# Memory key and value products, split by upper and lower 64 features onto two tiles of array rows

## The chip, the core and the metric

One core of a Trainium2 chip runs the whole program in one launch. The metric is the device time of that launch in microseconds (us). The kernel before takes 2544.36 us, the median of three runs (2544.34 to 2545.03).

## The reference, cut to what matters

The reference is a decoder trunk of four layers (256 positions, width 2048) that cycles through three attention mixers. Each layer also attends to a memory of 256 rows, whose keys and values come from one projection per layer. Only that projection is touched here:

```python
mem_n = _rmsnorm(mem, mem_norm)                       # (1, 256, 2048)
for i in range(DEPTH):                                # 4 layers
    ...
    mem_out = _memory_attention(mq, mem_n @ w_mem_kv[i])   # w_mem_kv[i]: (2048, 2048)
# first 1024 columns of the product: keys of 4 heads x 256; last 1024: values
```

## The kernel before

All numbers are 32-bit floats. Each operand of a large product is split into a high and a low part (`split`, L81: ScalarE makes the high part in the type `float32r`, VectorE subtracts it from the value for the low part), and a product is the sum of three: high by high, high by low, low by high. The contraction runs over 2048 features in 16 steps of 128, which are the 128 rows of TensorE's array.

`memory()` (L412 to L502) comes first and makes the keys and values of all four layers. For each layer and each half `p_` it makes one value product, then two key products:

- A value product (`rows_by`, L270) keeps memory features as the stationary operand and streams 512 columns of weights: six matmuls of 512 columns for each of 16 steps, into two PSUM banks (the tile `acc_mv`).
- A key product (`columns_by`, L294) keeps 128 weight columns as the stationary operand and streams the memory: for each step two matmuls of 512 columns (high weights by both parts of the memory, L310) and two of 256 (low weights by the high part, L314), into the two banks of `acc_mk`.

There are 8 value products and 16 key products. The first value product is special: it also prepares the memory's own parts while the first weights arrive.

Weights come by DMA in pieces of 512 KB (`stage`, L234, five buffers, issued on SP's queue). `parts_of` (L264) splits each piece of 128x512 into `wh` (ScalarE, L74) and `wl` (VectorE, L83), each with three buffers. TensorE reads them and so frees them. The kernel lays out eight PSUM banks: two pairs under the tag `acc` (one product fills a pair while the pair before is read out), and four single banks under the tag `mp` (`misc`, L57), which `memory()` uses only for `spread`.

When a key product ends, `keys` (L459) calls `total` (L341: ScalarE copies one half of each bank to `z`, VectorE adds the other), multiplies by a scale (L462), splits and sends the result to DRAM on GpSimd's queue. When a value product ends, `values` (L449) scales and splits it straight from PSUM. `spread` (L196) runs two small matmuls over all 128 rows: once for the memory's scales, and once, near the end of `memory()`, for the norm of layer 0.

Each engine works through its own queue in order. The framework's scheduler fixes that order when the program is built, by its own estimate of times, so that `wl` pieces for the next product stand between the steps that read out the last one.

Of the kernel before, what the change touches and what calls it, by code (L numbers as in the profile page):

```python
# [8 lines left out]
F32 = mybir.dt.float32  # L9
# [6 lines left out]
P = 128  # L16
S = 256
# [7 lines left out]
MEMW = 1024  # L25
ST = 2
N_TAB = 384
PQ, AUX, WR, PT, WARM = 5, 4, 5, 4, 11
# [17 lines left out]
def kernel(ctx: ExitStack, tc: tile.TileContext, a: dict, out: bass.AP,  # L46
                             kinds=(0, 1, 2, 0)):
    nc = tc.nc
# [3 lines left out]
    act = ctx.enter_context(tc.tile_pool(name="act", bufs=1))  # L52
    wk = ctx.enter_context(tc.tile_pool(name="wk", bufs=1))
    ps = ctx.enter_context(tc.tile_pool(name="ps", bufs=1, space=bass.MemoryType.PSUM))
    dr = ctx.enter_context(tc.tile_pool(name="dr", bufs=1, space=bass.MemoryType.DRAM))

    def misc(name, dt=F32):  # L57
        return ps.tile([P, 512], dt, name=name, tag="mp", bufs=4)
# [14 lines left out]
    def copy_act(o, i, scale=1.0):  # L73
        inst = nc.scalar.activation(o, i, AF.Copy, scale=scale)  # L74
        if pinned:
            tc.keep_in_program_order(inst)
# [182 lines left out]
    def other_work():  # L259
        for _ in range(2):  # L260
            if steps and next(steps[0], None) is None:
                steps.pop(0)

    def parts_of(wr, c0, n):  # L264
        wh = wp.tile([P, 512], F32R, name="wh", tag="wh", bufs=3)
        wl = wp.tile([P, 512], F32R, name="wl", tag="wl", bufs=3)
        split(wh[:, :n], wl[:, :n], wr[:, c0:c0 + n])
        return wh, wl

    def rows_by(xt, kts, w, k0, cols, name, prepare=None, each=None, exact_first=False):  # L270


        pair = ps.tile([P, 2, 512], F32, name=f"acc_{name}", tag="acc", bufs=2)
        acc = [pair[:, t, :] for t in range(2)]
        for s in range(0, kts, ST):
            m = min(ST, kts - s)
            wr, n = stage(w, k0 + s, m, cols, each)
            other_work()
            for k in range(m):
                if prepare is not None:  # L280
                    prepare(s + k)
                wh, wl = parts_of(wr, k * n, n)
                q = xt[(s + k) // 4]
                seq = [(t, v, w_) for t in range(2) for v, w_ in ((0, wh), (0, wl), (1, wh))]
                if exact_first:
                    seq.sort(key=lambda z: z[2] is wl)
                for n_, (t, v, w_) in enumerate(seq):
                    later = [z for z in seq[n_ + 1:] if z[0] == t]
                    nc.tensor.matmul(acc[t][:, :n], q[:, v, (s + k) % 4, t * P:(t + 1) * P], w_[:, :n],  # L289
                                     start=s + k == 0 and v == 0 and w_ is wh,  # L290
                                     stop=s + k == kts - 1 and not later)
        return pair

    def columns_by(xt, kts, w, k0, cols, name):  # L294

        pair = ps.tile([P, 2, 2, S], F32, name=f"acc_{name}", tag="acc", bufs=2)
        acc = [pair[:, j] for j in range(2)]
        for s in range(0, kts, 2 * ST):
            m = min(2 * ST, kts - s)
            wr, n = stage(w, k0 + s, m, cols)  # L300
            other_work()
            for k2 in range(0, m, 2):
                wh, wl = parts_of(wr, k2 * S, 2 * S)
                for k in range(2):
                    kt = s + k2 + k
                    q = xt[kt // 4]

                    for j in range(2):
                        o = k * S + j * P
                        nc.tensor.matmul(acc[j], wh[:, o:o + P], q[:, :, kt % 4, :],  # L310
                                         start=kt == 0, stop=False)
                    for j in range(2):
                        o = k * S + j * P
                        nc.tensor.matmul(acc[j][:, 0, :], wl[:, o:o + P], q[:, 0, kt % 4, :],  # L314
                                         start=False, stop=kt == kts - 1)
        return pair

    def columns_of(xt, kts, w, c0, tiles, name):
# [19 lines left out]
                                         q[:, 0, kt % 4, r0:], start=False, stop=kt == kts - 1)  # L338
        return pair, acc[2:]

    def total(pair, name="z"):  # L341
        z = tmp(name).rearrange("p (j c) -> p j c", j=2)
        copy_act(z, pair[:, :, 1, :])
        nc.vector.tensor_add(z, z, pair[:, :, 0, :])
        return z
# [66 lines left out]
    def memory():  # L412
        mrstd = cst.tile([P, 2], F32, name="mrstd")
        m16 = cst.tile([P, 2], F32, name="m16")
        mbc = act.tile([P, S], F32, name="mbc", tag="kr", bufs=1)
        mT = [act.tile([P, 2, 4, S], F32R, name="mT", tag=f"big{c}") for c in range(4)]
        mss = small("mss", 8, bufs=2)

        def each(k):

            if k == 1:
                mft[0].load(1)
            if k in (3, 7, 11):
                mft[k // 4 + 1].load(0, 4)
            if k == 15:
                tc.keep_in_program_order(nc.sync.dma_start(ident, a["c_ident"]))
                nc.vector.tensor_copy(identr, ident)

        def prepare(k):
            c = k // 4  # L430
            weighted_parts(mT[c], mft[c].q, k % 4, c * 4)

        def memory_rows(c):
            q = act.tile([P, 2, 512], F32, name="mrow", tag="pq", bufs=PQ)
            for t in range(2):
                tc.keep_in_program_order(
                    nc.sync.dma_start(q[:, t, :], min_[t][:, c * 512:(c + 1) * 512]))
            return q

        def row_scales(mrow):  # L440
            for c in range(4):
                for t in range(2):
                    square_sum(mss[:, t * 4 + c:t * 4 + c + 1], mrow[c][:, t, :])
            s2 = small("ms2", 2)
            nc.vector.tensor_reduce(s2, mss.rearrange("p (t c) -> p t c", t=2), AX.X, OP.add)
            rsqrt_mean(mrstd, s2, D)
            nc.vector.tensor_scalar(m16, mrstd, 0.0625, None, op0=OP.mult)

        def values(i, p_, acc):  # L449
            v = [act.tile([P, 2, 512], F32R, name="mv", tag="aux", bufs=AUX) for z in range(2)]  # L450
            for t in range(2):
                sc = mrstd[:, t:t + 1]
                copy_act(v[0][:, t, :], acc[:, t, :], scale=sc)
                nc.vector.scalar_tensor_tensor(v[1][:, t, :], acc[:, t, :], sc, f32(v[0])[:, t, :],
                                               op0=OP.mult, op1=OP.subtract)
            for z in range(2):
                nc.gpsimd.dma_start(mv[i][p_][:, z], v[z])

        def keys(i, h, acc):  # L459
            kT = act.tile([P, 2, 2, S], F32R, name="mkT", tag="pq", bufs=PQ)  # L460
            z = total(acc)
            nc.vector.tensor_mul(z, z, mbc[:, None, :].to_broadcast([P, 2, S]))  # L462
            split(kT[:, 0], kT[:, 1], z)
            nc.gpsimd.dma_start(mkT[i][h], kT)

        def first_keys(acc):
            yield True
            yield True
            spread(mbc, m16)
            keys(0, 0, acc)  # L470

        for i in range(depth):
            w = a["w_mem_kv"][i]
            for p_ in range(2):
                begins = i == p_ == 0
                if begins:

                    pinned.append(0)
                    acc = rows_by(mT, 16, w, 0, (MEMW, 512), "mv", prepare, each, True)
                    pinned.pop()  # L480
                    mrow = [memory_rows(c) for c in range(4)]
                    raw = act.tile([P, 2, 512], F32, name="raw", tag="aux", bufs=AUX)
                    for t in range(2):
                        copy_act(raw[:, t, :], acc[:, t, :])
                else:
                    values(i, p_, rows_by(mT, 16, w, 0, (MEMW + p_ * 512, 512), "mv"))
                for h in (2 * p_, 2 * p_ + 1):
                    acck = columns_by(mT, 16, w, 0, (h * 256, 256), "mk")
                    if begins and h == 0:
                        row_scales(mrow)  # L490
                        values(i, p_, raw)
                        steps.append(first_keys(acck))
                    else:
                        keys(i, h, acck)
                step = 2 * i + p_
                if begins:

                    not_before(f32(mT[3])[:, 0, 3, :1])
                    late_constants()
                    bias_tables()  # L500
                if 1 <= step < 5:
                    steps.append(nm.first_chunk(step - 1))  # L502
# [826 lines left out]
```

## Time and profile before

| | before |
|---|---|
| median of 3 runs | 2544.36 us |
| the profiled execution, whole | 2544.75 us |
| its span, first to last instruction | 2543.0 us |
| TensorE (PE) busy in the span | 2532.3 us, 100% |
| weight loads of the array (PEld) busy | 2184.4 us, 86% |
| VectorE (DVE) busy | 1889.3 us, 74% |
| ScalarE (ACT) busy | 1604.9 us, 63% |
| granted TensorE clock, mean | 0.999 |

PE is the matmul stream, PEld the loads of stationary operands, which the trace shows on a line of their own. Matmuls are pipelined: one lasts longer than the distance between two starts, so the cost of a matmul is read from starts, not from durations. An idle engine that nobody waits for costs nothing.

### The profile page before, as it was taken

The page shows a single profiled execution, that of the slowest core. Times are in us where ns is not written, and L with a number is a line of the kernel's source. Part 1 is how long each engine was busy: PE and PEld are TensorE (multiplying, and loading weights), DVE is VectorE, ACT ScalarE, POOL GpSimd, SP SyncE. Part 2 cuts the span into 40 slices and gives each one's busy share as a digit, 9 for nine tenths or more (in the row PEclk, how much of TensorE's full clock was granted, in tenths as well). Part 3 has the DMA queues.
Part 4 walks back from the last instruction along what each step waited for, and adds up shares of the span by engine and source line. Part 5 has one row for each costly group of instructions (what it writes and reads, how often), then busy time and mean ns, then how long its engine had stood idle before and what let it go on. Part 6 is the DMA issues. An engine that isn't in the chain of part 4 may idle for free.

```text
span 2543.0 us, 41598 instructions
## 1 busy us (share of the span) xinstructions
PE 2532.3 (100%) x14070; PEld 2184.4 (86%) x14070; DVE 1889.3 (74%) x3832; ACT 1604.9 (63%) x3291; POOL 95.9 (4%) x237
## 2 busy tenths in 40 slices
PE   9999999999999999999999999999999999999998
PEld 8888888888888889888888888888889888888887
DVE  6666666677777677988777777878868777777766
ACT  6556556556566556777666566667756666656655
POOL 1200000000000000000000000000000000000000
PEclk9999999999999999999999999999999999999999
DMA  9888777676677666766666565666656768666765
GB/s 306 258 265 259 248 213 236 174 190 179 184 191 208 198 194 192 216 188 176 191 186 186 170 219 176 178 179 176 197 157 176 227 185 221 191 193 188 220 172 185
DMA packets 478582, 511.67 MB, mean 201 GB/s; under 512 B 70656, under 2 KB 391040, under 8 KB 477728
## 3 DMA queue, kind: packets, MB, share of 16 engines
q1 hardware_dynamic: 461856, 451.82, 60.7%
q0 software_dynamic: 15792, 56.22, 7.0%
q8 instruction: 110, 1.80, 0.3%
q10 hardware_dynamic: 720, 0.98, 0.1%
q14 instruction: 104, 0.85, 0.1%
HBM read 483.67 MB, written 29.46 MB: 202 GB/s over the span
## 4 chain that ended last, share of the span: by engine, by line
PE 99%; DVE 0%; DMA 0%; ACT 0%; issue 0%; SPq 0%; DVEq 0%
PE acc_wo L289 20%; PE acc_g L310 14%; PE acc_g L314 7%; PE acc_mv L289 7%; PE acc_q L310 5%; PE acc_mq L310 5%; PE acc_mk L310 5%; PE acc_cq L310 4%; PE acc_qn L310 4%; PE acc_q L314 2%; PE acc_mq L314 2%; PE acc_mk L314 2%; PE acc_cq L314 2%; PE acc_qr L310 2%; PE acc_qn L314 2%; PE acc_va L289 2%
## 5 line engine op out<-in xcount | busy, mean ns | idle before, releaser
L74 ACT ACTIVATE wh<-wr 128x512 fp32r<-128x512 f32 (+1 forms) x1712 | 1064.9, 624 | 816.7 <-PE acc_g L310 143.3
L83 DVE TENSOR_TENSOR wl<-wr,wh 128x512 fp32r<-128x512 f32 (+1 forms) x1712 | 1155.0, 679 | 558.7 <-ACT wh L74 529.7
L310 PE MATMUL acc_g<-xT,wh 128*128 128x512 f32 x1536 | 483.8, 397 | 0.0
L289 PE MATMUL acc_wo<-wh,y 128*128 128x512 f32 x1504 | 473.1, 391 | 0.0
L314 PEld LDWEIGHTS acc_g<-xT,wl 128*128 128x128 f32 x1536 | 282.4, 188 | 62.7 <-DVE wl L83 0.9
L289 PEld LDWEIGHTS acc_wo<-wh,y 128*128 128x128 f32 x1504 | 282.4, 188 | 55.9
L314 PE MATMUL acc_g<-xT,wl 128*128 128x256 f32 x1536 | 304.8, 280 | 0.0
L289 PE MATMUL acc_wo<-wl,y 128*128 128x512 f32 x752 | 297.7, 396 | 0.0
L310 PEld LDWEIGHTS acc_g<-xT,wh 128*128 128x128 f32 x1536 | 235.4, 189 | 0.9
L289 PEld LDWEIGHTS acc_wo<-wl,y 128*128 128x128 f32 x752 | 141.3, 188 | 26.4
L310 PE MATMUL acc_q<-xT,wh 128*128 128x512 f32 x512 | 161.4, 396 | 0.0
L310 PE MATMUL acc_mq<-xT,wh 128*128 128x512 f32 x512 | 161.1, 396 | 0.0
L310 PE MATMUL acc_mk<-mT,wh 128*128 128x512 f32 x512 | 160.7, 395 | 0.0
L289 PE MATMUL acc_mv<-wh,mT 128*128 128x512 f32 x512 | 156.6, 390 | 1.7 <-ACT wh L74 1.7
L310 PE MATMUL acc_qn<-cT,wh 128*128 128x512 f32 x384 | 121.0, 396 | 0.0
L310 PE MATMUL acc_cq<-xT,wh 128*128 128x512 f32 x384 | 120.9, 396 | 0.0
L314 PEld LDWEIGHTS acc_mk<-mT,wl 128*128 128x128 f32 x512 | 95.8, 188 | 22.6 <-DVE wl L83 0.2
L289 PEld LDWEIGHTS acc_mv<-wh,mT 128*128 128x128 f32 x512 | 95.9, 188 | 22.2 <-ACT wh L74 2.7
L1248 DVE TENSOR_TENSOR xc<-xc,acc_wo 128x1024 f32<-128x1024 f32 x92 | 112.1, 1218 | 2.6 <-PE acc_wo L289 2.3
L314 PEld LDWEIGHTS acc_q<-xT,wl 128*128 128x128 f32 x512 | 94.7, 188 | 22.2 <-issue 0.7
L314 PEld LDWEIGHTS acc_mq<-xT,wl 128*128 128x128 f32 x512 | 94.8, 188 | 21.7 <-issue 0.2
L314 PE MATMUL acc_q<-xT,wl 128*128 128x256 f32 x512 | 102.2, 281 | 0.0
(332 smaller groups left out, 3833.2 us busy)
## 6 DMA issues: line engine op xcount, KB each, us to landing
wr<-in_w_out_dram SPq DMA_DIRECT2D x188, 512.0 KB, 3.8
wr<-in_w_in_a_dram SPq DMA_DIRECT2D x176, 512.0 KB, 4.3
wr<-in_w_mem_kv_dram SPq DMA_DIRECT2D x126, 512.0 KB, 4.7
wr<-in_w_in_b_dram SPq DMA_DIRECT2D x116, 512.0 KB, 3.6
wr<-in_w_in_c_dram SPq DMA_DIRECT2D x104, 512.0 KB, 3.5
wr<-in_w_uq_dram SPq DMA_DIRECT2D x288, 128.0 KB, 2.8
wr<-in_w_in_a_dram SPq DMA_DIRECT2D x32, 288.0 KB, 3.1
mv<-mv POOLq DMA_DIRECT2D x16, 512.0 KB, 6.6
```

What stands on the lines that cost most here:

```text
L74: inst = nc.scalar.activation(o, i, AF.Copy, scale=scale)
L83: nc.vector.tensor_sub(lo, src, f32(hi))
L289: nc.tensor.matmul(acc[t][:, :n], q[:, v, (s + k) % 4, t * P:(t + 1) * P], w_[:, :n], start=s + k == 0 and v == 0 and w_ is wh, stop=s + k ...
L310: nc.tensor.matmul(acc[j], wh[:, o:o + P], q[:, :, kt % 4, :], start=kt == 0, stop=False)
L314: nc.tensor.matmul(acc[j][:, 0, :], wl[:, o:o + P], q[:, 0, kt % 4, :], start=False, stop=kt == kts - 1)
L1248: nc.vector.tensor_add(xs, xs, acc)
```

## The change

Every value product but the first, and every key product, is cut in two over the contraction. Each matmul over 128 array rows becomes two matmuls over 64 rows: one at array rows 0 to 63, into the `acc` bank as before, and one at rows 64 to 127, into a bank of the tag `mp` (the tile `acb_...`). The same columns are streamed in both. At the end the two banks are added: for keys by four VectorE additions of 128x256 after `total`, for values by a ScalarE copy of both `acc` banks to a new tile `vr` and two VectorE additions of 128x512; `values` then reads `vr` instead of PSUM.

```diff
+    def row_halves(name, n):
+        pair = ps.tile([P, 2, 512], F32, name=f"acc_{name}", tag="acc", bufs=2)
+        banks = [pair[:, t, :] for t in range(2)], [misc(f"acb_{name}") for t in range(2)]
+
+        def product(t, l, r, start, stop):
+            width = r.shape[1] * (r.shape[2] if len(r.shape) == 3 else 1)
+            for z in range(2):
+                rows = slice(64 * z, 64 * z + 64)
+                nc.tensor.matmul(banks[z][t][:, :width], l[rows], r[rows], start=start, stop=stop,
+                                 tile_position=(64 * z, 0))
+        return pair, banks[1], product
+
+    def rows_in_halves(xt, kts, w, cols, name):
...
+                for t in range(2):
+                    for n_, (v, w_) in enumerate(((0, wh), (0, wl), (1, wh))):
+                        product(t, q[:, v, k % 4, t * P:(t + 1) * P], w_[:, :],
+                                k == n_ == 0, k == kts - 1 and n_ == 2)
+        return pair, more
+
+    def columns_in_halves(xt, kts, w, cols, name):
...
+                    for j in range(2):
+                        product(j, wh[:, k * S + j * P:k * S + j * P + P], q[:, :, kt % 4, :], kt == 0, False)
+                    for j in range(2):
+                        product(j, wl[:, k * S + j * P:k * S + j * P + P], q[:, 0, kt % 4, :],
+                                False, kt == kts - 1)
+        return pair, more
...
         def keys(i, h, acc):
-            z = total(acc)
+            z = total(acc[0].rearrange("p j (v c) -> p j v c", v=2))
+            for j in range(2):
+                for v in range(2):
+                    nc.vector.tensor_add(z[:, j, :], z[:, j, :], acc[1][j][:, v * S:(v + 1) * S])
...
-                    values(i, p_, rows_by(mT, 16, w, 0, (MEMW + p_ * 512, 512), "mv"))
+                    acc, more = rows_in_halves(mT, 16, w, (MEMW + p_ * 512, 512), "mv")
+                    vr = act.tile([P, 2, 512], F32, name="vr", tag="aux", bufs=AUX)
+                    copy_act(vr, acc)
+                    for t in range(2):
+                        nc.vector.tensor_add(vr[:, t, :], vr[:, t, :], more[t])
+                    values(i, p_, vr)
                 for h in (2 * p_, 2 * p_ + 1):
-                    acck = columns_by(mT, 16, w, 0, (h * 256, 256), "mk")
+                    acck = columns_in_halves(mT, 16, w, (h * 256, 256), "mk")
```

TensorE's queue at the start of the first key product, before: `acc_mk` is the pair of banks, `mT` the memory, `wh` and `wl` the parts of the weights, and the shape is that of the output.

```order
L310 MATMUL acc_mk_385<-mT_148,wh_388 128x512 x2
L314 MATMUL acc_mk_385<-mT_148,wl_389 128x256 x2
L310 MATMUL acc_mk_385<-mT_148,wh_388 128x512 x2
L314 MATMUL acc_mk_385<-mT_148,wl_389 128x256 x2
L310 MATMUL acc_mk_385<-mT_148,wh_400 128x512 x2
```

The same place after the change: `acb_mk` are the two further banks.

```order
L350 MATMUL acc_mk_385<-mT_148,wh_390 128x512
L350 MATMUL acb_mk_386<-mT_148,wh_390 128x512
L350 MATMUL acc_mk_385<-mT_148,wh_390 128x512
L350 MATMUL acb_mk_387<-mT_148,wh_390 128x512
L350 MATMUL acc_mk_385<-mT_148,wl_391 128x256
L350 MATMUL acb_mk_386<-mT_148,wl_391 128x256
L350 MATMUL acc_mk_385<-mT_148,wl_391 128x256
L350 MATMUL acb_mk_387<-mT_148,wl_391 128x256
```

Each matmul has become two that stand next to each other in the queue, one for each tile of rows; nothing else stands between them.

VectorE's queue where a key product ends and a value product begins (layer 0, last head), before: `z` is the tile that collects the keys, and the `wl` pieces are already those of the value product.

```order
L83 TENSOR_TENSOR wl_1194<-wr_1191,wh_1193 128x512
L344 TENSOR_TENSOR z_1156<-z_1156,acc_mk_1050 128x512
L462 TENSOR_TENSOR z_1156<-z_1156,mbc_147 128x512
L83 TENSOR_TENSOR wl_1204<-wr_1191,wh_1203 128x512
L83 TENSOR_TENSOR wl_1216<-wr_1213,wh_1215 128x512
```

The same place after the change.

```order
L83 TENSOR_TENSOR wl_1590<-wr_1587,wh_1589 128x512
L390 TENSOR_TENSOR z_1534<-z_1534,acc_mk_1362 128x512
L510 TENSOR_TENSOR z_1534<-z_1534,acb_mk_1363 128x256
L510 TENSOR_TENSOR z_1534<-z_1534,acb_mk_1364 128x256
L510 TENSOR_TENSOR z_1534<-z_1534,acb_mk_1363 128x256
L510 TENSOR_TENSOR z_1534<-z_1534,acb_mk_1364 128x256
L511 TENSOR_TENSOR z_1534<-z_1534,mbc_147 128x512
L83 TENSOR_TENSOR wl_1606<-wr_1587,wh_1605 128x512
```

The four additions have come between the third `wl` piece of the value product and the fourth. GpSimd's and SP's queues issue the same transfers; from layer 0's first product on, TensorE's queue is the same as before.

## Rows read from the trace of the kernel before

**Rows 1.** The page: busy time of the engines, and chain by engine.

```profile
PE 2532.3 (100%) x14070; PEld 2184.4 (86%) x14070; DVE 1889.3 (74%) x3832; ACT 1604.9 (63%) x3291; POOL 95.9 (4%) x237
...
PE 99%; DVE 0%; DMA 0%; ACT 0%; issue 0%; SPq 0%; DVEq 0%
```

**Rows 2.** Stretches: length, busy PE, PEld, DVE, ACT, POOL; clock, DMA share, GB/s.

```profile
52.36:74.14 21.78, 21.78 (x98) 18.02 (x97) 12.75 (x20) 11.14 (x18) 12.18 (x44) 1.00 0.83 259
74.14:96.43 22.29, 22.29 (x130) 19.45 (x128) 14.23 (x22) 12.36 (x21) 8.22 (x35) 1.00 0.87 266
...
140.48:361.01 220.53, 220.53 (x1125) 187.61 (x1123) 141.59 (x231) 125.61 (x216) 10.62 (x20) 1.00 0.79 248
361.01:2543.00 2181.99, 2174.08 (x12254) 1879.91 (x12252) 1656.43 (x3439) 1392.90 (x2917) 60.09 (x126) 1.00 0.66 191
```

**Rows 3.** Matmuls of both kinds of product by shape: count, busy us, mean ns.

```profile
L310 PE MATMUL acc_mk<-mT,wh 128*128 128x512 f32 x512 | 160.7, 395 | 0.0
L289 PE MATMUL acc_mv<-wh,mT 128*128 128x512 f32 x512 | 156.6, 390 | 1.7 <-ACT wh L74 1.7
L314 PE MATMUL acc_mk<-mT,wl 128*128 128x256 f32 x512 | 100.7, 278 | 0.0
L289 PE MATMUL acc_mv<-wl,mT 128*128 128x512 f32 x256 | 97.0, 389 | 0.0
```

**Rows 4.** Timeline of TensorE in a key product: start us, us, what.

```profile
130.03 0.63 PE L310 MATMUL acc_mk<-mT,wh 128*128 128x512 f32 x2
130.50 0.39 PE L314 MATMUL acc_mk<-mT,wl 128*128 128x256 f32 x2
130.73 0.63 PE L310 MATMUL acc_mk<-mT,wh 128*128 128x512 f32 x2
```

**Rows 5.** Timeline of the weight loads in the same stretch.

```profile
130.27 0.42 PEld L314 LDWEIGHTS acc_mk<-mT,wl 128*128 128x128 f32 x2
```

**Rows 6.** Matmuls on tiles of 64 array columns, layer 1's attention: mean ns.

```profile
L1081 PE MATMUL o<-pT,vs 128*64 128x384 f32 x64 | 13.2, 492 | 0.0
```

**Rows 7.** Timeline: two such matmuls, one on each tile.

```profile
1162.29 0.49 PE L1081 MATMUL o<-pT,vs 128*64 128x384 f32 x2
```

**Rows 8.** Timeline of TensorE into and out of these tiles.

```profile
1161.70 0.39 PE L314 MATMUL acc_q<-xT,wl 128*128 128x256 f32 x2
1162.02 0.44 PE L1081 MATMUL o<-pT,vh 128*64 128x128 f32 x4
1162.29 1.03 PE L1081 MATMUL o<-pT,vs 128*64 128x384 f32 x8
1163.15 0.61 PE L1081 MATMUL o<-pT,vh 128*64 128x128 f32 x8
1163.59 1.03 PE L1081 MATMUL o<-pT,vs 128*64 128x384 f32 x8
1164.45 0.39 PE L1081 MATMUL o<-pT,vh 128*64 128x128 f32 x4
1164.77 0.74 PE L310 MATMUL acc_q<-xT,wh 128*128 128x512 f32 x2
1165.35 0.40 PE L314 MATMUL acc_q<-xT,wl 128*128 128x256 f32 x2
```

**Rows 9.** Timeline of VectorE after a key product that ended at 140.48.

```profile
141.12 0.69 DVE L83 TENSOR_TENSOR wl<-wr,wh 128x512 fp32r<-128x512 f32 x1 [0.70 <-ACT wh L74]
141.73 0.68 DVE L344 TENSOR_TENSOR z<-z,acc_mk 128x512 f32<-128x512 f32 x1
142.44 0.69 DVE L462 TENSOR_TENSOR z<-z,mbc 128x512 f32<-128x512 f32 x1
143.05 0.69 DVE L83 TENSOR_TENSOR wl<-wr,wh 128x512 fp32r<-128x512 f32 x1
```

**Rows 10.** Timeline of TensorE: the matmul that first reads that last piece.

```profile
144.80 0.39 PE L289 MATMUL acc_mv<-wl,mT 128*128 128x512 f32 x1
```

**Rows 11.** An addition of 128x256 from PSUM elsewhere: count, busy us, mean ns.

```profile
L571 DVE TENSOR_TENSOR u<-sp,caus 128x256 f32<-128x256 f32 x32 | 13.4, 417 | 0.0
```

**Rows 12.** Timeline: two weight loads one after another, after the column tiles.

```profile
1164.77 0.30 PEld L310 LDWEIGHTS acc_q<-xT,wh 128*128 128x128 f32 x2 [0.17 <-issue]
```

More of the change, by code (lines that the diff above doesn't have):

```diff
@@ L339, in columns_of @@
         return pair, acc[2:]
+    def row_halves(name, n):
[9 more added lines that the diff above has]
+    def rows_in_halves(xt, kts, w, cols, name):
+        pair, more, product = row_halves(name, 512)
+        for s in range(0, kts, ST):
+            wr, n = stage(w, s, ST, cols)
+            other_work()
+            for k in range(s, s + ST):
+                wh, wl = parts_of(wr, (k - s) * n, n)
+                q = xt[k // 4]
+                for t in range(2):
[4 more added lines that the diff above has]
+    def columns_in_halves(xt, kts, w, cols, name):
+        pair, more, product = row_halves(name, 512)
+        for s in range(0, kts, 2 * ST):
+            wr, n = stage(w, s, 2 * ST, cols)
+            other_work()
+            for k2 in range(0, 2 * ST, 2):
+                wh, wl = parts_of(wr, k2 * S, 2 * S)
+                for k in range(2):
+                    kt = s + k2 + k
+                    q = xt[kt // 4]
+                    for j in range(2):
[4 more added lines that the diff above has]
+        return pair, more
     def total(pair, name="z"):
```

## The prediction, made before the changed kernel ran

> **What bounds the kernel now.** I read the page first. TensorE is busy for the whole span, and the chain that ended last lies on it for 99% [rows 1]. So time moves only where TensorE's own stream gets shorter, longer or is made to wait. Next comes the view by stretches. [...] VectorE has 12.8 to 14.2 us of work in such a stretch and ScalarE 11.1 to 12.4: both have room on the average. From layer 0's first product, at 361.01, nothing is changed on TensorE's queue, so the 2182 us after it stay [rows 2], and the question lies in the 309 us from the second value product on and in the first two key products.
>
> [...] The groups by shape give 768 matmuls for 8 value products, 96 each, and 1024 for 16 key products, 64 each [rows 3]. [...]
>
> [...] In the timeline of the loads, the first load for the low weights starts at 130.27, 0.01 us after the second of the matmuls that began at 130.03 (130.03 + 0.63 less one duration of 0.40, from the mean in [rows 3]), so it lies beside a whole matmul [rows 5]. [...]
>
> **The change, part by part.**
>
> *The products.* 7 x 96 + 16 x 64 = 1696 matmuls become 1696 pairs. No row shows tiles of array rows. The nearest rows are the tiles of array columns in layer 1's attention: one matmul of 384 columns lasts 492 ns [rows 6], and two of them, one on each tile, together 0.49 us from the first start to the last end [rows 7]: they run side by side. Eight matmuls (four of 384 columns, four of 128) lie between 1162.29 and 1163.15, and eight of 128 between 1163.15 and 1163.59 [rows 8]. That is 0.11 us per pair of 128 and (0.86 - 0.22) / 2 = 0.32 us per pair of 384. [...] One ns per pair is 1.7 us.
>
> *Changes between whole array and tiles.* Going in: from 1161.70 to 1162.29 there are two matmuls of 256 columns (0.23) and two pairs (0.22), yet 0.59 us pass: 0.14 is lost. Coming out: from 1164.45 to 1165.35, two pairs (0.22) and two matmuls of 512 (0.47) take 0.90: 0.21 is lost [rows 8]. The changed queue goes in after the first value product, out and in around the first `spread`, whose two matmuls stand together, out and in twice around the second, whose two stand apart, and out at layer 0: four times each way, 4 x 0.35 = 1.4 us. Bounds: 0 to 2.8, twice that.
>
> *Reading out a key product.* Here VectorE's room decides. Before, after a product that ended at 140.48, VectorE makes the third `wl` piece of the value product, adds, multiplies, and makes the fourth, ready at 143.05 + 0.69 = 143.74 [rows 9]; TensorE reads it at 144.80 [rows 10]. So 1.06 us are to spare. The change puts four additions of 128x256 in between. One takes 0.42 us [rows 11]. An instruction that does not read its predecessor's result starts 0.08 before its end (141.12 + 0.69 against 141.73), one that does 0.03 after it (141.73 + 0.68 against 142.44) [rows 9]. Three of the steps are of the first kind and the last, into the multiplication, is of the second: 3 x 0.34 + 0.45 = 1.47 us. That is 0.41 more than there is to spare, and TensorE, in order, stands still for it. There are seven such ends before a value product: 7 x 0.41 = 2.9 us. Bounds: 0.30 (all at 0.34) to 0.74 (all at 0.45) each, 2.1 to 5.2 us. Behind a key product followed by another key product, the order puts the multiplication after the fourth piece and the need comes later: nothing. Behind a value product the copy to `vr` and two additions of 0.68 (as L344 in [rows 9]) stand before the third `wl` piece. No row here gives the spare time; I bound it by 0 and the 0.74 of a key product's end, seven times 0 to 5.2 us, and take 0, as the copy falls while VectorE has nothing urgent. The banks themselves wait for nobody: the next product has the other pair and the other two of `mp`.
>
> *Sum.* Against the profiled execution, 2544.75 us (span 2543.0 and 1.75 around it; the median of the runs is 0.39 less): 2544.75 + 0 + 1.4 + 2.9 = 2549.05. I say **2549 us**, 0.2% over the median. About 0.2%, 5.1 us, is what a measurement of this kernel can tell from no change, so this stands near that edge.
>
> **Rivals.**
>
> [...]
> [...]
>
> *The two tiles' loads go one after another, or hold up both streams (slower).* A load occupies the array for 0.11 us: two in a row last 0.30, and one 0.19 (0.42 for two less the 0.23 between their starts) [rows 5, 12]. Two per pair are 0.22, less than a matmul of 512 columns, but 0.10 more than one of 256 (0.23 / 2 [rows 4]). It decides from the point where the two loads of a pair outlast its matmul: the 512 pairs of 256 columns, + 51 us, 2544.75 + 51 + 4.3 = 2600. [...] For it: twice as many loads in the same time. Against it: the column tiles also load twice per pair, within 0.11 us per pair of 128 [rows 8].
> [...]
>
> *The pairs do not run side by side at all* (the change does not do what it says): 7 x 21.78 + 8 x 22.29 = 331 us more, 2880. Against it speak the column tiles [rows 7].
>
> **How the numbers follow.** Pairs like single matmuls: 0.48, own range 2546 to 2554 (a ns per pair either way, the bounds of the stalls), about half of it within 0.2% of before and half above. Gap gone: 0.30, faster. Gap doubled: 0.10; loads in a row: 0.07; nothing side by side: 0.05; all slower. So faster 0.30, same 0.25, slower 0.45. The range leaves out the two dearest cases (0.12) and a part of the tails: 2526 to 2576.
>
> **What would show it.** [...] A load on one tile that starts only when the other's has ended shows the loads in a row. Idle time of TensorE before the fourth `wl` of each value product, some 0.4 us, shows the read-out; none there refutes it. A change of the times after 361 us that is not a plain shift would make the whole account wrong.

## The result, and the profile after

The changed kernel takes 2569.65 us (median of 4 runs, 2567.91 to 2571.09) against 2544.44 us for the kernel before (4 runs, 2544.34 to 2545.03): ratio 1.0099, interval 1.0083 to 1.0115, slower by 25.2 us. It is slower, as forecast, but by five times as much: 20.6 us over the 2549. The spans of the two profiled executions differ by 26.3 us (2569.3 for 2543.0).

The page of the kernel after, busy time and the chain that ended last, against [rows 1]:

```profile
PE 2550.9 (99%) x15766; PEld 2197.0 (86%) x15766; DVE 1919.0 (75%) x3910; ACT 1604.0 (62%) x3298; POOL 95.0 (4%) x237
...
PE 96%; DVE 2%; DMA 1%; ACT 1%; issue 0%; POOL 0%; SPq 0%; DVEq 0%; ACTq 0%
```

Three per cent of the chain have left TensorE, most of it for VectorE and a DMA. The timeline of the kernel after, inside a split value product, tells whether the pairs are to blame:

```profile
120.03 0.39 PE L350 MATMUL acc_mv<-wh,mT 64*128 64x512 f32 x1
120.03 0.39 PE L350 MATMUL acb_mv<-wh,mT 64*128 64x512 f32 x1
120.03 0.18 PEld L350 LDWEIGHTS acc_mv<-wh,mT 64*128 64x128 f32 x1
120.03 0.18 PEld L350 LDWEIGHTS acb_mv<-wh,mT 64*128 64x128 f32 x1
120.25 0.39 PE L350 MATMUL acc_mv<-wh,mT 64*128 64x512 f32 x1
120.26 0.39 PE L350 MATMUL acb_mv<-wh,mT 64*128 64x512 f32 x1
```

They are not: two pairs stand 0.22 to 0.23 us apart, both tiles start together, and so do their loads, which last 0.18 us each. The view by stretches says where the time is; its columns are those of [rows 2].

```profile
29.27:54.33 25.06, 23.59 (x261) 19.78 (x261) 19.27 (x45) 14.38 (x29) 1.74 (x3) 1.00 0.78 251
54.33:84.28 29.95, 25.26 (x196) 20.96 (x194) 13.88 (x24) 10.98 (x18) 17.77 (x75) 0.89 0.60 193
...
107.39:129.77 22.38, 22.32 (x196) 18.06 (x194) 14.78 (x25) 12.18 (x21) 0.53 (x1) 1.00 0.81 262
...
267.01:294.02 27.01, 26.99 (x260) 22.63 (x258) 20.57 (x49) 14.96 (x27) 1.59 (x3) 1.00 0.65 210
...
385.24:2569.30 2184.06, 2174.81 (x12254) 1880.05 (x12252) 1658.54 (x3443) 1389.48 (x2917) 60.11 (x126) 1.00 0.64 191
```

Two stretches of the kernel before that [rows 2] leaves out, the first pair of key products and the pair with the second `spread`:

```profile
29.76:52.36 22.60, 22.60 (x132) 19.63 (x130) 17.66 (x41) 14.72 (x29) 1.74 (x3) 1.00 0.89 286
250.36:272.88 22.52, 22.52 (x131) 19.70 (x130) 17.89 (x43) 14.21 (x27) 1.59 (x3) 1.00 0.83 262
```

The first split value product takes 29.95 us for 21.78, the first two key products 25.06 for 22.60 (layer 0's `spread` of the memory's scale lies there), the two key products with the second `spread` 27.01 for 22.52; the other six value products gain 0.60 us each and the six other pairs of key products 0.8 to 1.1. From layer 0 on it is 2.1 us more. The waits of the weight loads from 29 to 385 us name the engine (us in total, times, the longest):

```profile
PEld acc_mv L350 <- DVE wl L83: 9.6, 15, 5.1
PEld acc_mk L350 <- DVE wl L83: 7.7, 20, 0.6
PEld acc_mk L350 <- ACT wh L74: 3.2, 7, 1.5
```

Before, this list held one wait of 0.2 us. The longest is seen on VectorE, with TensorE's stall below it (two timelines of the kernel after):

```profile
61.22 0.69 DVE L83 TENSOR_TENSOR wl<-wr,wh 128x512 fp32r<-128x512 f32 x1 [0.20 <-ACT wh L74]
68.68 0.17 DVE L145 TENSOR_SCALAR nsink<-nsink 128x16 f32<-128x16 f32 x1 [6.76 <-DMA nsink<-in_l_sinks_dram]
```

```profile
69.50 0.79 PE L350 MATMUL acc_mv<-wl,mT 64*128 64x512 f32 x1 [4.65 <-DVE wl L83]
```

VectorE comes to `nsink` at 61.9 us, before GpSimd has issued its transfer (63.7 us, 4.6 us to landing), and stands there for 6.76 us. These are sixteen numbers per row that nobody reads before 1592.6 us, and every `wl` piece is queued behind them. TensorE, idle for 4.65 us, comes back at a granted clock of 0.50, as the stretch right after it shows, and is back at 1.00 in the stretch from 76 to 78 us (0.50 from 72 to 74, 0.71 from 74 to 76):

```profile
70.00:72.00 2.00, 2.00 (x12) 1.53 (x10) 0.65 (x2) 0.00 (x0) 2.00 (x14) 0.50 0.75 197
```

Before, the same instruction stood five `wl` pieces later, was reached at 67.5 us (transfer issued at 60.9) and waited for nothing:

```profile
67.46 0.17 DVE L145 TENSOR_SCALAR nsink<-nsink 128x16 f32<-128x16 f32 x1
```

VectorE's order at that place (first before, then after), from the order of the built programs:

```
L83 TENSOR_TENSOR mkT<-z,mkT 128x512
L83 TENSOR_TENSOR wl<-wr,wh 128x512 x8
L145 TENSOR_SCALAR nsink<-nsink 128x16
```

```
L83 TENSOR_TENSOR mkT<-z,mkT 128x512
L83 TENSOR_TENSOR wl<-wr,wh 128x512 x3
L145 TENSOR_SCALAR nsink<-nsink 128x16
```

In the first pair of key products it is ScalarE's order. The scaling of the first values (`mv<-raw,mrstd`) stands ahead of a `wh` piece and waits 2.65 us for VectorE's `mrstd`; TensorE stands 1.5 us for that `wh`. Before, it stood four `wh` pieces later and waited for nothing (first after, then before):

```profile
35.89 1.34 ACT L74 ACTIVATE mv<-raw,mrstd 128x512 fp32r<-128x512 f32 x2 [2.65 <-DVE mrstd L192]
```

```profile
38.69 1.33 ACT L74 ACTIVATE mv<-raw,mrstd 128x512 fp32r<-128x512 f32 x2
```

And the end of a key product that a value product follows, in the timeline of VectorE after:

```profile
154.38 0.68 DVE L390 TENSOR_TENSOR z<-z,acc_mk 128x512 f32<-128x512 f32 x1
155.09 1.42 DVE L510 TENSOR_TENSOR z<-z,acb_mk 128x256 f32<-128x256 f32 x4
156.54 0.69 DVE L511 TENSOR_TENSOR z<-z,mbc 128x512 f32<-128x512 f32 x1
157.15 0.68 DVE L83 TENSOR_TENSOR wl<-wr,wh 128x512 fp32r<-128x512 f32 x1
```

The four additions cost 1.45 us on VectorE, as forecast (1.47), and hold the `wl` piece back by as much. Where another key product follows, the additions end at 144.67, and this comes next:

```profile
144.58 0.68 DVE L83 TENSOR_TENSOR wl<-wr,wh 128x512 fp32r<-128x512 f32 x1
145.18 0.69 DVE L511 TENSOR_TENSOR z<-z,mbc 128x512 f32<-128x512 f32 x1
146.56 0.69 DVE L83 TENSOR_TENSOR mkT<-z,mkT 128x512 fp32r<-128x512 f32 x1 [0.70 <-ACT mkT L74]
147.17 1.89 DVE L83 TENSOR_TENSOR wl<-wr,wh 128x512 fp32r<-128x512 f32 x3
```

The fourth `wl` piece comes in time, but ScalarE waits 2.6 us for the multiplication, with `wh` pieces behind it, and the fifth `wl` piece stands behind `mkT`. TensorE loses some 0.7 us between 146.74 and 148.13.

### The profile page after: what moved, and what is told of

Same layout as the page of the kernel before. It is cut to its first block, busy times and chain, and to the rows that moved or that the text cites. A ratio compares the mean times of both kernels' runs of the same rounds, so it can differ in the third digit from the quotient of the medians.

```text
span 2569.3 us, 45073 instructions
## 1 busy us (share of the span) xinstructions
PE 2550.9 (99%) x15766; PEld 2197.0 (86%) x15766; DVE 1919.0 (75%) x3910; ACT 1604.0 (62%) x3298; POOL 95.0 (4%) x237
## 4 chain that ended last, share of the span: by engine, by line
PE 96%; DVE 2%; DMA 1%; ACT 1%; issue 0%; POOL 0%; SPq 0%; DVEq 0%; ACTq 0%
PE acc_wo L289 20%; PE acc_g L310 13%; PE acc_g L314 7%; PE acc_mk L350 5%; PE acc_q L310 5%; PE acc_mq L310 5%; PE acc_cq L310 3%; PE acc_qn L310 3%; PE acc_mv L350 3%; PE acc_q L314 2%; PE acc_mq L314 2%; PE acb_mv L350 2%; PE acc_cq L314 2%; PE acc_qr L310 2%; PE acc_qn L314 2%; PE acc_va L289 2%
## 5 line engine op out<-in xcount | busy, mean ns | idle before, releaser
L310 PE MATMUL acc_g<-xT,wh 128*128 128x512 f32 x1536 | 483.8, 397 | 0.0
L310 PEld LDWEIGHTS acc_g<-xT,wh 128*128 128x128 f32 x1536 | 235.4, 189 | 0.9
L350 PE MATMUL acc_mk<-mT,wh 64*128 64x512 f32 x512 | 161.0, 394 | 1.8 <-ACT wh L74 1.3
L350 PE MATMUL acb_mk<-mT,wh 64*128 64x512 f32 x512 | 161.5, 394 | 0.0
L310 PE MATMUL acc_q<-xT,wh 128*128 128x512 f32 x512 | 161.4, 396 | 0.0
L310 PE MATMUL acc_mq<-xT,wh 128*128 128x512 f32 x512 | 161.1, 396 | 0.0
L350 PE MATMUL acc_mv<-wh,mT 64*128 64x512 f32 x448 | 140.4, 391 | 0.0
L350 PE MATMUL acb_mv<-wh,mT 64*128 64x512 f32 x448 | 140.4, 391 | 0.0
L310 PE MATMUL acc_qn<-cT,wh 128*128 128x512 f32 x384 | 121.0, 396 | 0.0
L310 PE MATMUL acc_cq<-xT,wh 128*128 128x512 f32 x384 | 120.8, 396 | 0.0
L350 PEld LDWEIGHTS acc_mk<-mT,wl 64*128 64x128 f32 x512 | 92.7, 184 | 25.3 <-DVE wl L83 7.7
```

The lines of the kernel that those rows point to most:

```text
L350: nc.tensor.matmul(banks[z][t][:, :width], l[rows], r[rows], start=start, stop=stop, tile_position=(64 * z, 0))
```

## The experiments

### Is it the read-out, the wait for `nsink`, or something else?

My first theory: the pairs cost nothing, and the 25 us are VectorE's new work standing ahead of `wl` pieces. Three kernels were to show it.

`e1_no_readout`, the changed kernel without reading the second banks:

```diff
-            for j in range(2):
-                for v in range(2):
-                    nc.vector.tensor_add(z[:, j, :], z[:, j, :], acc[1][j][:, v * S:(v + 1) * S])
...
-                    values(i, p_, vr)
+                    values(i, p_, acc)
```

> The changed kernel with all 23 products still split on two tiles of array rows, but the second pair of banks is never read: keys leave out the four adds, values leave out the copy and the two adds (so the upper 64 features are missing from the output). Theory (pairs cost what one matmul cost; the 25 us are work of VectorE that stands ahead of the next wl piece): the waits of the product ends go, some 8 x (0.6 + 0.35 + 0.7) = 13 us, the wait for nsink (one stall of about 4.7 us and 2.4 us at the lower clock behind it) may stay, so 2551 to 2558 us; pairs start 227 ns apart on one tile as in the changed kernel. Rival (the pairs themselves, their loads or the changes of tile mode carry the 25 us): nothing to win, 2566 to 2571 us.

Measured: 2561.18 us (5 runs), ratio 1.0064 (1.0051 to 1.0077). It lies between the two: the read-out takes away 8.5 us and not 13.

`e2_nsink`, the changed kernel with the negation on GpSimd; on VectorE's queue nothing else moves:

```diff
-        nc.vector.tensor_scalar(nsink, nsink, -1.0, None, op0=OP.mult)
+        nc.gpsimd.tensor_scalar(nsink, nsink, -1.0, None, op0=OP.mult)
```

> The changed kernel, complete, with only the negation of nsink moved from VectorE to GpSimd, which issued that tile's transfer. Theory: VectorE no longer waits 6.8 us there, TensorE's stall of 4.7 us in the first split value product and the half clock behind it (2.4 us) go: 2562 us (2560 to 2564). Rival (the stall only takes the place of one that comes later anyway): 2567 to 2570 us.

Measured: 2561.84 us, ratio 1.0068 (1.0055 to 1.0080). As expected: 7.8 us are this one instruction's place, and the first split value product falls to 22.39 us:

```profile
54.14:76.53 22.39, 22.36 (x197) 18.02 (x194) 14.00 (x23) 10.98 (x18) 8.23 (x25) 1.00 0.77 253
```

`e5_readout_only`, the kernel before with the additional read-out alone:

```diff
             z = total(acc)
+            for j in range(2):
+                for v in range(2):
+                    nc.vector.tensor_add(z[:, j, :], z[:, j, :], acc[:, j, v, :])
...
```

> The kernel before, no tile of array rows anywhere, with the changed kernel's extra read-out alone: four more adds of 128x256 behind each of 16 key products, one copy of 128x1024 and two adds of 128x512 behind each of 7 value products, taken from the banks that are there (the sums are then not the reference's). Theory: the read-out alone makes most of what is left when the wait for nsink is taken out, +10 to +16 us, 2555 to 2560 us, with the waits for wl at the ends of products. Rival (pairs, loads or tile mode carry it): the adds are hidden as VectorE is busy three quarters of the time, +0 to +3 us, 2544 to 2547 us.

Measured: 2545.26 us (11 runs), ratio 1.0003 (0.9994 to 1.0011). My theory falls: the same additions, on an engine just as busy, cost 0.7 us, and the interval has room for nothing at all. So it is not VectorE's load. Stretches of this kernel, the first pair of key products, a value product and the pair after it, and the pair with the second `spread`:

```profile
30.25:52.83 22.58, 22.58 (x131) 19.62 (x130) 18.95 (x45) 14.76 (x29) 1.74 (x3) 1.00 0.89 285
185.25:207.02 21.77, 21.77 (x98) 18.02 (x97) 14.74 (x25) 12.30 (x21) 0.53 (x1) 1.00 0.84 276
207.02:229.38 22.36, 22.36 (x129) 19.38 (x128) 17.44 (x30) 14.55 (x27) 1.59 (x3) 1.00 0.81 248
251.15:273.76 22.61, 22.61 (x132) 19.64 (x131) 19.75 (x49) 14.90 (x28) 1.59 (x3) 1.00 0.77 241
```

VectorE has 17.44 us of work in the third, more than before ([rows 2]: 14.23), and TensorE never stands still. What differs from the changed kernel is the place of the work. There the four additions stand in a row; here they have `wl` pieces between them, and the small steps of the memory's scale too. Of VectorE's first 482 instructions 234 stand elsewhere in the changed kernel than in this one, of ScalarE's first 375, 112, and after that none.

### The order of the queues

New theory: the change costs what the scheduler's new order of VectorE's and ScalarE's queues costs. Two kernels swap the orders. A table gives the order of up to 490 of VectorE's and 384 of ScalarE's first instructions, and the program is built with it:

```diff
...
+def queue_orders(tc):
+    traced = list(tc.nc.cur_bb.bb.instructions)
+    for engine, ranks in ORDERS:
+        mine = [i for i in traced if engine in str(i.engine)]
+        for p_, q in zip(ranks, ranks[1:]):
+            tc.add_manual_dep(mine[q], mine[p_].name,
+                              mybir.DependencyInfo(mybir.DependencyClass.NoSync,
+                                                   mybir.DependencyReason.DATA),
+                              reason="queue_orders")
...
```

`e6_order` is the changed kernel in the order of `e5_readout_only` (but for 14 places of VectorE and 7 of ScalarE around the second `spread`).

> The changed kernel, complete, with all 23 split products and the whole read-out, but VectorE's and ScalarE's queues put in the order in which they stand in the kernel of the last experiment (before plus the read-out, 2545.3 us): there the scale's small steps, the read-out's adds and nsink's negation stand between other wl and wh pieces. Theory (new, after the read-out by itself cost 0.7 us: what costs is the order that the change gives the two queues, and pairs cost what one matmul cost): 2545 to 2548 us, no wait of VectorE for nsink, no stall over 0.3 us at the ends of products. Rival (pairs leave TensorE less slack, so that the same read-out costs 8 us or more with them, or the changes of tile mode do): 2555 to 2562 us.

`e9_order_alone` is `e5_readout_only` in the order of the changed kernel (but for the order of the four additions among themselves and a few places at the end).

> The mirror of it: no tile of array rows anywhere; the kernel before plus the read-out (its sums are then not the reference's; 2545.3 us in the last experiments), with VectorE's and ScalarE's queues in the order of the changed kernel through the whole stretch of memory products. Theory (order of the queues): most of the 25 us come without any pair, 2562 to 2570 us, with VectorE's wait of 6 to 7 us for nsink and the lower clock behind it, the stall of 1.3 to 1.5 us in the first key product, and 0.4 to 0.7 us at the ends of products. Rival (pairs carry what is not nsink): 2550 to 2554 us, nsink's 7.8 us alone.

Measured: `e6_order` 2551.12 us, ratio 1.0026 (1.0016 to 1.0036); `e9_order_alone` 2571.89 us, ratio 1.0108 (1.0094 to 1.0121). The second settles it: without a single tile of rows, the order alone costs 26.6 us over `e5_readout_only`, and leaves the same marks: the waits of its loads, and its longest stretch (its lines lie 47 further down, so L130 is `wl`, L336 a value matmul):

```profile
PEld acc_mv L336 <- DVE wl L130: 12.8, 15, 5.1
PEld acc_mk L361 <- DVE wl L130: 8.7, 22, 0.8
PEld acc_mk L357 <- ACT wh L121: 7.5, 10, 1.9
```

```profile
55.21:85.33 30.12, 24.97 (x99) 19.65 (x97) 14.08 (x24) 11.01 (x18) 17.67 (x75) 0.89 0.61 194
```

`e6_order` gives back 18.5 of the 25.2 us. Two of its key products with their halves split cost just what `e5_readout_only`'s whole ones do, and only one stretch is long:

```profile
184.33:206.11 21.78, 21.78 (x196) 18.61 (x194) 14.74 (x25) 12.34 (x21) 0.53 (x1) 1.00 0.87 281
206.11:228.46 22.35, 22.35 (x259) 21.17 (x256) 17.46 (x30) 14.56 (x27) 1.60 (x3) 1.00 0.76 247
250.25:277.75 27.50, 27.50 (x263) 23.71 (x260) 20.32 (x49) 15.00 (x27) 1.60 (x3) 1.00 0.67 214
```

### The halves that came apart

The timeline of `e6_order` in that long stretch (L399 is the changed kernel's L350, L253 its `spread`):

```profile
264.23 0.63 PE L399 MATMUL acc_mk<-mT,wh 64*128 64x512 f32 x2
264.70 0.39 PE L399 MATMUL acc_mk<-mT,wl 64*128 64x256 f32 x2
264.93 0.62 PE L399 MATMUL acc_mk<-mT,wh 64*128 64x512 f32 x2
265.39 0.39 PE L399 MATMUL acc_mk<-mT,wl 64*128 64x256 f32 x2
265.71 0.38 PE L253 MATMUL spr<-dgr,onesr 128*128 128x256 f32 x1
266.03 0.74 PE L399 MATMUL acb_mk<-mT,wh 64*128 64x512 f32 x2
266.61 0.40 PE L399 MATMUL acb_mk<-mT,wl 64*128 64x256 f32 x2
```

Here nothing runs side by side: matmuls of the tile at rows 0 to 63 alone (`acc_mk`), the `spread`, then those of the tile at rows 64 to 127 alone (`acb_mk`), each at the pace of a whole one (0.47 us for two of 512 columns and 0.23 for two of 256, as in [rows 4]). In the changed kernel the halves come apart too, from 278.8 us on. Why is counted from the code and not read from a trace: the `mp` tag has four banks; the product that just ended holds two, `spread` takes one, and the next product finds one where it needs two. The scheduler has put the `acc` halves ahead.

`e10_order_together`: the whole order of `e5_readout_only` (with the same `spread` later), the halves pinned together, and `spread` later so that it takes its bank last.

```diff
+        first = [1]
...
+                inst = nc.tensor.matmul(banks[z][t][:, :width], l[rows], r[rows], start=start, stop=stop,
+                                        tile_position=(64 * z, 0))
+                if not first or z:
+                    tc.keep_in_program_order(inst)
+            first.clear()
...
             if c == 3:
+                for _ in range(2):
+                    yield True
                 self.finish()
```

> The kernel with the queues put in order (2551.1 us), complete, with two more edits: the second matmul of each pair is pinned behind the first on TensorE's queue, and the layer scale's spread is emitted one stage of weights later, so that it takes its PSUM bank after the next product has its own two. In the last kernel's trace the first key product past 250 us takes 27.5 us instead of 22.5: around the spread, matmuls of the lower rows run for 3.8 us by themselves (233 and 115 ns apart) and then those of the upper rows by themselves. Theory (those halves that were not side by side are all that was left): 5 us less, 2545 to 2547 us, that product at 22.4 to 23 us. Rival (halves cost more in some other way, or the wait for the bank takes the place): 2549 to 2553 us.

`e11_together`: these two edits alone on the changed kernel.

> The changed kernel with these two edits alone (pairs pinned together, the spread one stage later), VectorE's and ScalarE's queues left to the planner, which orders them nearly as in the changed kernel. Theory: only the 4 to 5 us of the product around the spread come back: 2564 to 2567 us, with nsink's wait and the stalls at the ends of products as they are. Rival (halves that come apart are the cause of more than that): 2560 us or less. Second rival (there the order of the queues costs the same 4 to 5 us by itself, and the halves apart only hide behind it): 2568 to 2571 us.

Measured: 2552.43 us, ratio 1.0031 (1.0018 to 1.0043), and 2567.81 us, ratio 1.0091 (1.0077 to 1.0105). The first misses: my pin also held all later matmuls behind `spread`, and TensorE stood there; the row of `e10_order_together` shows 1.78 us without work, and a lower clock:

```profile
260.00:270.00 10.00, 8.22 (x84) 6.79 (x82) 7.79 (x27) 4.07 (x7) 0.00 (x0) 0.95 0.79 258
```

The second comes back by 1.8 us, between the two expectations; its stretch by 2.85 (24.16 for 27.01). So most of the slowdown is not there.

`e12_order_loose` takes away the part of the pin that did harm:

```diff
-                if not first or z:
+                if z:
```

> The last kernel in order (2552.4 us) with one pin less: the second matmul of a pair still stands right behind the first, but a product's matmuls may pass the scale's spread on TensorE's queue. In the last trace TensorE stood 1.6, 1.2, 1.0 and 1.0 us before the two spreads' matmuls for dgr, since all behind them was pinned there, and the clock was lower for a while after; the product around the second spread took 26.7 us, and the one around the first 24.7. Theory (the order of the queues, and the halves that came apart, are all): 2545 to 2548 us, those products at 22.4 to 23.3 us, no stall over 0.4 us. Rival (a pair around a change of tile mode, or the bank that spread and halves share, costs the 5 us in whatever order): 2550 to 2553 us.

Measured: 2546.77 us (11 runs) against 2544.55, ratio 1.0009 (1.0000 to 1.0018). The stretches with the two `spread` (the first and the last line), two value products and a pair of key products:

```profile
29.30:52.57 23.27, 23.27 (x260) 20.36 (x261) 18.96 (x45) 14.66 (x29) 1.74 (x3) 1.00 0.83 276
52.57:74.13 21.56, 21.56 (x195) 18.42 (x193) 13.85 (x24) 11.08 (x18) 9.42 (x33) 1.00 0.84 262
140.60:162.39 21.79, 21.79 (x197) 21.79 (x195) 14.71 (x26) 12.34 (x21) 0.53 (x1) 1.00 0.86 280
162.39:184.75 22.36, 22.36 (x260) 20.34 (x258) 17.52 (x30) 14.54 (x27) 1.59 (x3) 1.00 0.77 248
250.66:274.05 23.39, 23.39 (x261) 19.80 (x258) 19.84 (x49) 14.88 (x28) 1.59 (x3) 1.00 0.70 229
```

The change, complete, with its read-out, costs 2.2 us when VectorE's and ScalarE's queues stand in the order of `e5_readout_only`, the halves stay together and the second `spread` comes later.

### The parts alone, and a layout that won nothing

`e3_values_only` and `e4_keys_only` split the values or the keys alone, in the scheduler's order.

> The changed kernel with the values' 7 products split and the keys' 16 as before. Its VectorE queue has nsink's negation 3 wl pieces behind the key read-out, as in the changed kernel (before: 8). Theory: nsink's 7 to 8 us, and 7 ends of value products of some 0.35 us: 2554 us (2552 to 2557). Rival (pairs carry what is not nsink, by their share of TensorE's time, 0.46 of 17 us): 2560 us.

> The changed kernel with the keys' 16 products split and the values' 7 as before. nsink's negation stands 8 wl pieces behind the key read-out, as in the kernel before. Theory: no wait for nsink; the adds of the keys' read-out stand in two pieces with a wl between, so less than the 0.56 and 0.70 us at the ends of key products, and the stalls at the two spreads: 2550 us (2546 to 2556). Rival (pairs carry what is not nsink, by share 0.54 of 17 us): 2554 us, without stalls at the ends of products.

Measured: 2554.32 us, ratio 1.0037 (1.0024 to 1.0051), as the theory said; and 2558.27 us, ratio 1.0055 (1.0041 to 1.0069), 2 us over its upper end. In the second, the key products carry 0.9 us a pair and the two at `spread` 2.6 and 4.3. Here `nsink` stands where it stood before; with the values split it moves. 9.6 and 13.5 us add up to 23.1 of 25.2.

`e7_contig` tried for a version that beats both, on the kernel before:

```diff
-        mT = [act.tile([P, 2, 4, S], F32R, name="mT", tag=f"big{c}") for c in range(4)]
+        mT = [act.tile([P, 4, 2, S], F32R, name="mT", tag=f"big{c}").rearrange("p k v s -> p v k s") for c in range(4)]
...
```

`xT` and `cT` are laid out in the same way.

> The kernel before with one other layout: xT, mT and cT hold the two 256-column parts of a feature block side by side, so that the moving operand of the 512-column matmuls of L310 is one piece of 512 and not two pieces of 256. In the trace of before those matmuls start 233 ns apart and the ones of L289, with one piece of 512, 227 ns; about 2,090 of L310 have such a record. Theory (the second piece costs the 6 ns): 2,090 x 6.3 ns = 13 us less, 2531 us. Rival (it is the stationary operand or the change between wh and wl that costs them): no change, 2544 us, still 233 ns apart. Second rival: the writes of these tiles, now at a stride of 512, cost VectorE or ScalarE more and give it back: 2544 us or over, but 227 ns apart.

Measured: 2544.53 us, ratio 1.0000 (0.9991 to 1.0009), and the matmuls of L310 still start around 233 ns apart (230 to 236), as before. The two pieces of the moving operand are not what costs the 6 ns; what does stays open.

## Why the prediction fell short, step by step

The wide range, 2526 to 2576, holds the 2569.65, but by luck: it reached so far for slower cases, among them the one that the chances call "Gap doubled", and none of them occurred. The range of the case that did occur, pairs like single matmuls, was 2546 to 2554, and the result is 15.7 us over it.

- **Products: right.** A pair costs what one matmul cost. With the read-out in both, two key products take 22.36 us split (`e12_order_loose`) and 22.36 whole (`e5_readout_only`), a value product 21.79 and 21.77. On one tile, starts of 512 columns stand 227 ns apart (4.08 us for 18 from 119.80 on, at a granted clock of 1.00), as whole ones did before (21.78 us for 96, [rows 2]). The loads of both tiles start together at 120.03 and neither waits for the other's. No row stood behind the 0 us that the sum has for the products; these times are what the runs gave in its place. Nor does a run show the gap that two of the chances name, a time that a matmul takes beyond its columns: what the runs show is a distance of starts that stayed the same.
- **Changes between whole array and tiles: the size holds.** 1.4 us were forecast. What `e12_order_loose` has over `e5_readout_only` at the two `spread` is 0.69 and 0.78 us (22.58 and 22.61 us there); 0.22 of the first is in the value product behind it, which begins before that stretch ends and shows 21.56 us for 21.78. That leaves some 1.25 us. That it is the change of mode, and not the bank, was not taken apart.
- **Read-out: the step that failed, at two of its three kinds of end.** A key product before a value product was about right: 0.41 us forecast, 0.60 measured, within the bounds of 0.30 to 0.74. "Behind a key product followed by another key product [...] nothing" and the 0 behind a value product were wrong: the six other pairs of key products, which hold one end of each, gained 0.8 to 1.1 us a pair, 5.8 in all. In the pair from 129.77 on TensorE loses some 0.7 us at the first kind of end and 0.35 at the second. With the six value products (6 x 0.60) that is 9.4 us, where 2.9 stood in the sum. The work was sized well (1.47 forecast, 1.45 measured); its place was not: the order was read rightly, the multiplication behind the fourth `wl` piece, but when TensorE needs the fifth piece, and ScalarE's next `wh`, was not worked out. In another order the same work costs 0.7 us.
- **What the sum did not have at all.** `nsink` moved ahead of five `wl` pieces (7.8 us, `e2_nsink`); ScalarE's scaling of the first values, waiting for the scale's small steps on VectorE, moved ahead of `wh` pieces in the first key products, where 2.5 us were lost; at the second `spread` halves apart and the order together cost 4.5 (the order alone 3.3: 25.84 us in `e9_order_alone`). The prediction went over TensorE's queue from end to end, over VectorE's at the ends of products alone, and not over ScalarE's.
- **"The banks themselves wait for nobody": wrong, as far as the count goes,** at the second `spread`, which needs a fifth bank of the four under `mp`.
- **After 361 us: 2.1 us, not settled.** This stretch is 2182.0 us before, 2184.1 after, and in single traces of the other kernels 2182.0 (`e9_order_alone`) to 2184.4 (`e6_order`). The loads of `acc_g` wait for `wl` for 3.0 us in all, for 0.9 before; 1.8 of it is in layer 0, where there was no such wait. `e9_order_alone`, in the same order, has 1.1, so the order alone does not make it. The cause was not tried. The prediction had named a change behind 361 us as a sign against its whole account; for these 2.1 us that stays unanswered.

Why the scheduler moves this work when halves stand in TensorE's queue was not shown; only that it does, and what it costs.

## What to carry to other kernels

Where a scheduler orders the queues, a change on one engine can re-time all of them, and the cost may come from instructions that the diff never touches: compare the whole order of every engine that feeds the bottleneck, and for each moved instruction ask when its input lands and what is queued behind it. To part the work from its place, build the work alone, then the old code in the new order: here that gave 0.7 and 26.6 us. Before splitting accumulators, count the banks at the moment when a third user holds one.

## What the hardware showed

- Two tiles of 64 array rows ran side by side at the time of one whole matmul: in the changed kernel pairs of 512 columns start 227 ns apart, as whole ones did before, and both tiles' loads of 128 columns start together and last 0.18 us each.
- A lone matmul on 64 rows took as long as a whole one: 0.47 us for two of 512 columns at 264.23 in `e6_order`, as in [rows 4].
- An idle TensorE of 4.65 us cost more than itself: the granted clock then was 0.50 from 70 to 74 us. Moving the one waiting instruction to GpSimd gave 7.8 us.
